# Where the RG-LRU pieces of the output projection stand among the attention heads, and when the second half of W_out is loaded

## The chip, the core and the metric

The kernel runs on one core of a Trainium2 chip. The metric is the device time of one execution in microseconds (us): the median of the runs. Five engines work side by side, each on its own instructions in a fixed order: PE (TensorE, the matmuls), DVE (VectorE), ACT (ScalarE), POOL (GpSimd) and SP (SyncE, which here only issues transfers). A wait of one engine for another is a semaphore.

## The reference

One block of a streaming encoder with a sequence of 1024 tokens and a model width of 1024, all in float32:

```python
x   = layer_norm(alpha*x + 0.5*swiglu(x, ffn1...))
z   = x @ w_in                                    # q, k, v, lru input, lru gate, forget gate
fox = forgetting_attention(q, k, v, fg)           # 8 heads of 64, causal
#     logit[t,s] = q_t.k_s/8 + cum_t - cum_s ;  softmax over s <= t ;  times v
lru = gelu(z_gate) * rg_lru(conv(z_x))            # 512 channels
x   = layer_norm(alpha*x + concat([fox, lru]) @ w_out)
x   = layer_norm(alpha*x + 0.5*swiglu(x, ffn2...))
```

The change sits in the line with `w_out`: the product has an lru half (rows 512 to 1023 of `w_out`) and a fox half (rows 0 to 511).

## The kernel before, in words

Every float32 product is made of three fp32r matmuls (`mm3`, L151 to L153) on operands that were split into a high and a low part: ACT copies the high part, DVE subtracts it from the source to get the low part. The two feed-forward blocks take most of the time and are not touched. Between them stand the input projection with the RG-LRU (`mixer_in`) and `attention`.

`attention` walks over 64 units. A unit is one head `h` and one block `i` of 128 query rows, which looks at `i + 1` blocks of keys; heads 0 to 5 take `i` from 7 down to 0, so unit number n is head n // 8 for the first 48, and units 48 to 63 mix heads 6 and 7. At step n of the loop stand, in this order:

- `probs` for unit n: score matmuls into a PSUM tile `s` of two (L967, L968); on POOL an affine select that masks a block of `cum` (L971); on DVE the sum with `cum` and its minimum (L973, tile `p`, scalars `m`); on ACT the exponential with the row sum (L974); on DVE a reciprocal (L975); on POOL the scaling of `p` (L976).
- `to_pT` for unit n - 3: PE transposes `p` (L987), ACT and DVE split the result into `pt` (L991, L992).
- `values` for unit n - 4 where its `i` is even: PE multiplies `pt` with `v` (L1003), ACT and DVE put the result into `o` (L1006, L1007); after an odd head both are split into `mix` (L1010, L1011), and the pair's `mix` is stored to memory by POOL (L1014, `mix_d`).
- at some steps a piece of the lru half of the output projection: `down_tile` for one block of 128 rows and half of the columns. A piece is 12 matmuls of 128x512 (L151 to L153, `a<-w,mix`) and one DVE addition of the sum to the residual row (L213). There are 16 pieces. They stand at steps 0 and 1 and wherever n % 8 is 2, 3 or 4, until they run out at step 35:

```python
fill = [(i, d) for i in range(NT) for d in range(2)]
...
if fill and (n < 2 or n % 8 in (2, 3, 4)):
    i, d = fill.pop(0)
    with self.tc.issue_after(scores.ins) if n < 3 else nullcontext():
        self.down_tile(i, lru_tiles, 1.0, (d,))
```

- at steps 45, 47, 49 and 51 one step of `out_w` for the fox half of `w_out`: it loads 1 MB into one of two `raw` buffers (every second step) and splits 128 rows of it (ACT L143, DVE L144, 128x1024). The eight `ws` buffers that the splits write, and the eight `h` buffers into which `mix` comes back from memory (SP, L1062), hold the lru half until the last piece has read it.
- loads of the next head: q, kh, kl twice each, `cum`, `v` (SP, L950 to L955), into two sets of buffers.

From unit 57 on stand the pieces of the fox half (also L151 to L153), each pair followed by the layer norm of a row block; then the second feed-forward block, whose first weights (L255, `raw`) SP already loads during attention, when the `raw` buffers are free.

A scheduler that runs when the program is built puts the instructions of each engine into their final order; the text above gives it the sequence to start from. It may move a transfer or a transpose ahead or back by some units.

Of the kernel before, what the change touches and what calls it, by code (L numbers as in the profile page):

```python
# [24 lines left out]
FOX = 512  # L25
# [23 lines left out]
def f32(ap):  # L49
    return ap.bitcast(F32)  # L50


class Block:
# [866 lines left out]

    def out_w(self, w_out, row0):

        wv = w_out.rearrange("(f p) d -> p f d", p=P)
        for c in range(2):
            r = self.raw([P, 2, D])
            f0 = row0 // P + 2 * c
            self.nc.sync.dma_start(r, wv[:, f0:f0 + 2, :])
            for j in range(2):  # L930
                yield tuple(t[:, 0, :] for t in self.split_ws(r[:, j:j + 1, :], 1))

    def attention(self, w_out, mixp, ln, normed):

        nc, v = self.nc, self.nc.vector
        mm = nc.tensor.matmul
        lru_w, (last_hi, last_lo) = self.out_w(w_out, FOX), self.marks
        lru_tiles = list(zip(self.mix_lru[0:2], lru_w))
        with self.tc.issue_after(last_hi.ins), self.tc.issue_after(last_lo.ins):
            lru_tiles += list(zip(self.mix_lru[2:4], lru_w))  # L940
        with self.pool("att_p", 3) as pp, self.pool("att_t", 1) as tp, self.pool("att_pt", 6) as ptp, self.pool("att_qk", 2, side="right") as qkp:

            def load(h):
                vt = qkp.tile([P, NT, P], F32R, tag="v", name=self.nm("v"))
                cum = qkp.tile([P, T], F32, tag="cum", name=self.nm("cum"))
                q, kh, kl = (qkp.tile([P, T], F32R, tag=t, name=self.nm(t)) for t in ("q", "kh", "kl"))
                mine = slice(64 * (h % 2), 64 * (h % 2) + 64)
                for j in range(2):
                    rows = slice(64 * j, 64 * j + 64)
                    nc.sync.dma_start(f32(q[rows]), self.q_d[h // 2, j, mine, :])  # L950
                    nc.sync.dma_start(f32(kh[rows]), self.k_d[h // 2, 0, mine, :])
                    nc.sync.dma_start(f32(kl[rows]), self.k_d[h // 2, 1, mine, :])
                row = self.cum_d[h:h + 1, :]
                nc.sync.dma_start(cum, bass.AP(tensor=row.tensor, offset=row.offset, ap=[[0, P], [1, T]]))
                nc.sync.dma_start(f32(vt), self.v_d[h].rearrange("(j p) d -> p j d", p=P))  # L955
                return q, kh, kl, vt, cum

            def probs(h, i):

                q, kh, kl, _, cum = heads[h]  # L960
                n = (i + 1) * P
                ts = slice(i * P, n)
                s = self.s_tile()
                for bank in range((n + H - 1) // H):
                    c1 = min(max(n - bank * H, 256), H)
                    cols = slice(bank * H, bank * H + c1)
                    mm(s[:, bank, 0:c1], q[:, ts], kh[:, cols], start=True, stop=False)  # L967
                    scores = mm(s[:, bank, 0:c1], q[:, ts], kl[:, cols], start=False, stop=True)  # L968
                sf = s.rearrange("p b c -> p (b c)")
                p = pp.tile([P, T], F32, tag="p", name=self.nm("p"))  # L970
                nc.gpsimd.affine_select(cum[:, ts], cum[:, ts], pattern=[[-1, P]], compare_op=ALU.is_ge, fill=1e30, base=0, channel_multiplier=1)  # L971
                m = self.small.tile([P, 4], F32, tag="m", name=self.nm("m"))
                v.tensor_tensor_reduce(p[:, 0:n], sf[:, 0:n], cum[:, 0:n], 1.0, 3e38, ALU.add, ALU.min, m[:, 1:2])  # L973
                nc.scalar.activation(p[:, 0:n], p[:, 0:n], AF.Exp, bias=m[:, 1:2], scale=-1.0, accum_out=m[:, 2:3])  # L974
                v.reciprocal(m[:, 3:4], m[:, 2:3])  # L975
                nc.gpsimd.tensor_scalar(p[:, 0:n], p[:, 0:n], m[:, 3:4], 1.0, op0=ALU.mult, op1=ALU.mult)  # L976
                return p, scores

            def to_pT(h, i, p):
                if i % 2:  # L980
                    pts[h, i // 2] = [tuple(ptp.tile([P, 4, 256], F32R, tag="pt", name=self.nm("pt")) for _ in range(2))
                                      for _ in range((i + 4) // 4)]
                for g in range((i + 4) // 4):
                    js = range(4 * g, min(4 * g + 4, i + 1))
                    pa = self.a_tile()
                    for j in js:
                        nc.tensor.transpose(pa[:, (j % 4) * P:(j % 4 + 1) * P], p[:, j * P:(j + 1) * P], self.ident)  # L987
                    w = len(js)
                    pav = pa.rearrange("p (j t) -> p j t", j=4)[:, 0:w, :]
                    hi, lo = (x[:, 0:w, (i % 2) * P:(i % 2 + 1) * P] for x in pts[h, i // 2][g])  # L990
                    nc.scalar.copy(hi, pav)  # L991
                    v.tensor_tensor(lo, pav, f32(hi), ALU.subtract)  # L992

            def values(h, qt):
                vt = heads[h][3]
                b = h % 2
                rows, rest = slice(64 * b, 64 * b + 64), slice(64 - 64 * b, P - 64 * b)
                pv = self.a_tile()
                last = 2 * qt + 1
                for j in range(last + 1):  # L1000
                    ps = slice(P, 256) if j == last else slice(0, 256)
                    for l in range(2):
                        mm(pv[:, ps], vt[:, j, :], pts[h, qt][j // 4][l][:, j % 4, ps], start=j == 0 and l == 0, stop=j == last and l == 1)  # L1003
                cols = slice(qt * 256, (qt + 1) * 256)
                t = outs[h // 2]
                nc.scalar.copy(t[rows, cols], pv[rest, 0:256])  # L1006
                v.tensor_tensor(t[rows, cols], t[rows, cols], pv[rows, 0:256], ALU.add)  # L1007
                if b:
                    hi, lo = (x[:, cols] for x in mixes[h // 2])
                    nc.scalar.copy(hi, t[:, cols])  # L1010
                    v.tensor_tensor(lo, t[:, cols], f32(hi), ALU.subtract)  # L1011
                    if qt == 0 and h < HEADS - 1:
                        for l in range(2):
                            nc.gpsimd.dma_start(mix_d[h // 2][l], f32(mixes[h // 2][l]))  # L1014
# [3 lines left out]
            units = [(h, i) for h in range(HEADS - 2) for i in reversed(range(NT))]  # L1018
            units += [(6 + h, i) for h, i in ((0, 7), (0, 6), (0, 5), (0, 4), (1, 7), (1, 6), (0, 3), (0, 2),
                                              (1, 5), (1, 4), (0, 1), (0, 0), (1, 3), (1, 2), (1, 1), (1, 0))]  # L1020
            tiles, mix, w_fox, w_steps = [], [], [], self.out_w(w_out, 0)
            MIXES = 46, 48, 52
            fill = [(i, d) for i in range(NT) for d in range(2)]
            AHEAD = 3
            heads[0] = load(0)
# [8 lines left out]
            for n in range(len(units) + AHEAD + 1):  # L1034
                if n < len(units):
                    h, i = units[n]
                    if i == 5 and h < 6 or (h, i) == (6, 6):
                        heads[h + 1] = load(h + 1)
                    if i == NT - 1:
                        if h % 2 == 0:  # L1040
                            outs[h // 2] = tp.tile([P, T], F32, tag="o", name=self.nm("o"))
                        else:
                            mixes[h // 2] = tuple(mixp.tile([P, T], F32R, tag="h", name=self.nm("mix")) for _ in range(2))
                    ps[n], scores = probs(h, i)
                if 0 <= n - AHEAD < len(units):
                    to_pT(*units[n - AHEAD], ps.pop(n - AHEAD))
                if 0 <= n - AHEAD - 1 < len(units):
                    h, i = units[n - AHEAD - 1]
                    if i % 2 == 0:
                        values(h, i // 2)  # L1050
                        if h == HEADS - 1:
                            tiles += [(i + 1, 0), (i + 1, 1), (i, 0), (i, 1)]
                if fill and (n < 2 or n % 8 in (2, 3, 4)):
                    i, d = fill.pop(0)
                    with self.tc.issue_after(scores.ins) if n < 3 else nullcontext():
                        self.down_tile(i, lru_tiles, 1.0, (d,))
                if 45 <= n < 53 and n % 2:
                    w_fox.append(next(w_steps))
                if n in MIXES:
                    mix.append(tuple(self.hp.tile([P, T], F32R, tag="h", name=self.nm("mix")) for _ in range(2)))  # L1060
                    for l in range(2):
                        nc.sync.dma_start(f32(mix[-1][l]), mix_d[len(mix) - 1][l])  # L1062
                    if len(mix) == 3:
                        self.load_gb(*ln, [self.hp.tile([P, T], F32, tag="h", name=self.nm("gb")) for _ in range(2)])
                if tiles:
                    out_tile()
# [134 lines left out]
```

## Time and profile before

| | us |
|---|---|
| median of 3 runs | 2349.59 |
| lowest to highest | 2349.21 to 2351.27 |
| profiled execution, its own time | 2347.14 |
| its span, first to last instruction | 2345.4 |
| PE busy in the span | 2304.1 |
| DVE busy | 1631.6 |
| ACT busy | 1011.6 |
| POOL busy | 223.5 |

The profiled execution is 2.45 us below the median of the timed runs. Between its span and its own time lie 1.74 us. The heads' score matmuls start at 1209.02 us of the span (head 1) and the first piece of the fox half starts at 1343.03 us. In this text a head's time runs from the first score matmul of its first unit to that of the next head's.

### The profile page before, as it was taken

How to read it: one execution, taken by the hardware profiler on the slowest of the kernel's cores; microseconds unless marked ns; L12 is line 12 of the kernel's file. 1: busy time of each engine (PE TensorE's matmuls, PEld its weight loads, DVE VectorE, ACT ScalarE, POOL GpSimd, SP SyncE). 2: the span in 40 equal slices, each digit the busy share in tenths (PEclk: the TensorE clock that was granted, in tenths of full speed). 3: DMA queues.
4: the chain of work that ended last, by engine and by line, in shares of the span. 5: the costliest groups of instructions: out<-in, count | busy, mean ns of one | idle time of the engine just before them, and what ended most of it. 6: DMA issues, size and time to landing. Idle time of an engine off the chain costs nothing.

```text
span 2345.4 us, 28311 instructions
## 1 busy us (share of the span) xinstructions
PE 2304.1 (98%) x10721; PEld 1915.8 (82%) x10721; DVE 1631.6 (70%) x2512; ACT 1011.6 (43%) x1587; POOL 223.5 (10%) x364
## 2 busy tenths in 40 slices
PE   9999999999999999999999899999999999999997
PEld 7788888888888888888888777888888888788886
DVE  7766565666567888866667899665656566468787
ACT  5443333433344345454556745433333343344341
POOL 0020000000000000011134410000000000000000
PEclk9999999999999999999999999999999999999999
DMA  3433232323376434132366812232323232564532
GB/s 116 144 88 122 96 120 86 117 86 117 132 254 209 168 108 127 55 109 91 113 185 156 231 63 82 98 117 86 122 95 121 86 117 86 201 247 155 196 108 90
DMA packets 175832, 298.93 MB, mean 127 GB/s; under 512 B 8192, under 2 KB 100672, under 8 KB 175696
## 3 DMA queue, kind: packets, MB, share of 16 engines
q1 hardware_dynamic: 152624, 218.15, 29.1%
q0 software_dynamic: 23072, 78.97, 9.1%
q8 instruction: 84, 1.38, 0.3%
q14 instruction: 52, 0.43, 0.1%
HBM read 214.22 MB, written 82.87 MB: 127 GB/s over the span
## 4 chain that ended last, share of the span: by engine, by line
PE 87%; DVE 5%; issue 4%; DMA 2%; ACT 1%; POOL 1%; SPq 0%; POOLq 0%; ACTq 0%; DVEq 0%
PE x L153 9%; PE x L151 9%; PE x L152 9%; PE b L152 7%; PE b L153 7%; PE b L151 7%; PE s L153 6%; PE s L152 6%; PE s L151 6%; PE a L152 5%; PE a L151 5%; PE a L153 5%; PE a L1003 1%; PE a L987 1%; PE s L967 1%
## 5 line engine op out<-in xcount | busy, mean ns | idle before, releaser
L273 ACT CAST ws<-t 128x512 fp32r<-128x512 f32 x240 | 148.9, 623 | 389.3 <-PE b L152 268.8
L273 ACT CAST ws<-raw 128x512 fp32r<-128x512 f32 x180 | 111.8, 623 | 259.0 <-PE x L152 257.8
L274 DVE TENSOR_TENSOR ws<-raw,ws 128x512 fp32r<-128x512 f32 x180 | 123.9, 688 | 142.8 <-ACT ws L273 139.4
L274 DVE TENSOR_TENSOR ws<-t,ws 128x512 fp32r<-128x512 f32 x240 | 164.4, 686 | 70.5 <-ACT ws L273 68.5
L151 PE MATMUL b<-As,ws 128*128 128x512 f32 x512 | 199.8, 390 | 2.8 <-ACT As L309 2.6
L151 PE MATMUL a<-ws,ws 128*128 128x512 f32 x512 | 199.2, 390 | 2.1 <-ACT ws L607 1.6
L151 PE MATMUL x<-As,ws 128*128 128x512 f32 x512 | 199.6, 390 | 1.1 <-ACT ws L273 1.0
L153 PE MATMUL x<-As,ws 128*128 128x512 f32 x512 | 199.4, 390 | 0.7 <-DVE ws L274 0.6
L152 PE MATMUL a<-ws,ws 128*128 128x512 f32 x512 | 199.5, 390 | 0.5 <-DVE ws L608 0.5
L152 PE MATMUL b<-As,ws 128*128 128x512 f32 x512 | 199.4, 389 | 0.2 <-DVE As L315 0.2
L153 PE MATMUL b<-As,ws 128*128 128x512 f32 x512 | 199.4, 389 | 0.0
L152 PE MATMUL x<-As,ws 128*128 128x512 f32 x512 | 199.2, 389 | 0.0
L153 PE MATMUL a<-ws,ws 128*128 128x512 f32 x512 | 199.2, 389 | 0.0
L153 PE MATMUL x<-A,ws 128*128 128x512 f32 x496 | 193.2, 390 | 0.9 <-DVE ws L315 0.7
L151 PE MATMUL x<-A,ws 128*128 128x512 f32 x496 | 193.2, 389 | 0.8 <-ACT ws L273 0.8
L152 PE MATMUL x<-A,ws 128*128 128x512 f32 x496 | 193.0, 389 | 0.0
L607 ACT CAST ws<-raw 128x1024 fp32r<-128x1024 f32 x112 | 117.4, 1050 | 161.3 <-PE a L152 87.6
L543 POOL DMA_DIRECT2D h_d<-row x96 | 69.0, 721 | 1157.1 <-DVE row L537 1118.0
L608 DVE TENSOR_TENSOR ws<-raw,ws 128x1024 fp32r<-128x1024 f32 x112 | 136.5, 1220 | 53.9 <-ACT ws L607 53.0
L151 PE MATMUL s<-ws,ws 128*128 128x512 f32 x384 | 149.5, 389 | 0.0
L153 PE MATMUL s<-ws,ws 128*128 128x512 f32 x384 | 149.4, 389 | 0.0
L152 PE MATMUL s<-ws,ws 128*128 128x512 f32 x384 | 149.4, 389 | 0.0
(248 smaller groups left out, 5229.9 us busy)
## 6 DMA issues: line engine op xcount, KB each, us to landing
raw<-h_d SPq DMA_DIRECT2D x56, 1024.0 KB, 5.5
h_d<-row POOLq DMA_DIRECT2D x96, 512.0 KB, 3.7
wd<-in_ffn_w_down_dram SPq DMA_DIRECT2D x32, 1024.0 KB, 7.8
raw<-in_ffn_w_gate_dram SPq DMA_DIRECT2D x30, 1024.0 KB, 5.4
raw<-in_ffn_w_up_dram SPq DMA_DIRECT2D x30, 1024.0 KB, 5.4
h_d<-row POOLq DMA_DIRECT2D x32, 256.0 KB, 2.7
raw<-in_w_in_dram SPq DMA_DIRECT2D x16, 512.0 KB, 5.2
row<-in_x_dram SPq DMA_DIRECT2D x12, 512.0 KB, 8.9
```

Of the source, the lines that this page charges most:

```text
L151: mm(out, ah, bh, start=first, stop=False, skip_group_check=goes_on)
L152: mm(out, ah, bl, start=False, stop=False, skip_group_check=goes_on)
L153: mm(out, al, bh, start=False, stop=last, skip_group_check=goes_on)
L273: nc.scalar.copy(hi, src)
L274: v.tensor_tensor(lo, src, f32(hi), ALU.subtract)
L543: nc.gpsimd.dma_start(d[:, 2 * n:2 * n + 2], t.rearrange("p (r t) -> p r t", r=2))
L607: nc.scalar.copy(hi, src)
L608: self.mark = v.tensor_tensor(lo, src, f32(hi), ALU.subtract)
L967: mm(s[:, bank, 0:c1], q[:, ts], kh[:, cols], start=True, stop=False)
L987: nc.tensor.transpose(pa[:, (j % 4) * P:(j % 4 + 1) * P], p[:, j * P:(j + 1) * P], self.ident)
L1003: mm(pv[:, ps], vt[:, j, :], pts[h, qt][j // 4][l][:, j % 4, ps], start=j == 0 and l == 0, stop=j == last and l == 1)
```

## The change

The 16 pieces get a list of steps of their own: `FILLS`. Steps 0 to 4 keep their pieces; the other eleven stand at 8, 12 and 15 (head 1), 19 and 22 (head 2), 26 and 29 (head 3), 33 and 36 (head 4), 40 and 43 (head 5), where before they stood at 10, 11 and 12, 18, 19 and 20, 26, 27 and 28, 34 and 35. The loading of `w_out` is taken out of `out_w`; the fox half's two loads are written at steps 10 and 17 instead of 45 and 49, and its splits stay at 45, 47, 49 and 51.

```diff
-    def out_w(self, w_out, row0):
+    def out_raws(self, w_out, row0):
...
             self.nc.sync.dma_start(r, wv[:, f0:f0 + 2, :])
+            yield r
+
+    def out_w(self, raws):
+
+        for r in raws:
             for j in range(2):
                 yield tuple(t[:, 0, :] for t in self.split_ws(r[:, j:j + 1, :], 1))
...
-        lru_w, (last_hi, last_lo) = self.out_w(w_out, FOX), self.marks
+        lru_w, (last_hi, last_lo) = self.out_w(self.out_raws(w_out, FOX)), self.marks
...
-            tiles, mix, w_fox, w_steps = [], [], [], self.out_w(w_out, 0)
+            tiles, mix, w_fox, fox_raws = [], [], [], []
+            fox_loads, w_steps = self.out_raws(w_out, 0), self.out_w(fox_raws)
             MIXES = 46, 48, 52
+            FILLS = 0, 1, 2, 3, 4, 8, 12, 15, 19, 22, 26, 29, 33, 36, 40, 43
...
-                if fill and (n < 2 or n % 8 in (2, 3, 4)):
+                if n in (10, 17):
+                    fox_raws.append(next(fox_loads))
+                if n in FILLS:
                     i, d = fill.pop(0)
```

The line numbers of the changed kernel are 5 higher in this part of the loop (L967 becomes L972, and so on), and 9 higher from the place of the pieces on (L1062 becomes L1071).

On SP the two loads of the fox half (`raw`, L929) keep the rows that they had: the first stands ahead of head 0's loads, the second ahead of head 2's, in both kernels. What moves on SP is what stands around the loads of heads 6 and 7 (the two sets that follow each other from here; in both kernels `v` ends a head's set). SP before, from the `v` of head 6 to the `cum` of head 7, with the second feed-forward block's weights between them:

```order
L955 DMA v_10840<-v_d 128x8x128
L255 DMA raw_12046<-in_ffn_w_gate_dram 128x4x256
L255 DMA raw_12047<-in_ffn_w_up_dram 128x4x256
L255 DMA raw_12046<-in_ffn_w_gate_dram 128x4x256
L950 DMA q_11086<-q_d 64x1024
L951 DMA kh_11087<-k_d 64x1024
L952 DMA kl_11088<-k_d 64x1024
L950 DMA q_11086<-q_d 64x1024
L951 DMA kh_11087<-k_d 64x1024
L952 DMA kl_11088<-k_d 64x1024
L954 DMA cum_11085<-cum_d 128x1024
```

SP of the change, the same place:

```order
L960 DMA v_10830<-v_d 128x8x128
L1071 DMA mix_11015<-mix_d 128x1024
L1071 DMA mix_11016<-mix_d 128x1024
L1071 DMA mix_11082<-mix_d 128x1024
L1071 DMA mix_11083<-mix_d 128x1024
L956 DMA kh_11089<-k_d 64x1024
L955 DMA q_11088<-q_d 64x1024
L957 DMA kl_11090<-k_d 64x1024
L955 DMA q_11088<-q_d 64x1024
L956 DMA kh_11089<-k_d 64x1024
L957 DMA kl_11090<-k_d 64x1024
L959 DMA cum_11087<-cum_d 128x1024
```

Between the sets of heads 6 and 7 stood three weight loads, and now four loads of `mix`, which before stood ahead of head 6's set. The weight loads stand behind head 7's `cum`.

On DVE the splits of the fox half (L144) stood behind the score rows of units 35, 37, 39 and 42, and stand behind those of units 43, 45, 47 and 50. DVE before, from just behind the score row of unit 51 to that of unit 52, the first of head 7 (its operand is `s_11204`):

```order
L975 RECIPROCAL m_11146<-m_11146 128x1
L992 TENSOR_TENSOR pt_11170<-a_11173,pt_11169 128x4x128
L975 RECIPROCAL m_11164<-m_11164 128x1
L992 TENSOR_TENSOR pt_11172<-a_11180,pt_11171 128x4x128
L1007 TENSOR_TENSOR o_10498<-o_10498,a_11187 64x256
L992 TENSOR_TENSOR pt_11170<-a_11218,pt_11169 128x4x128
L1011 TENSOR_TENSOR mix_10787<-o_10498,mix_10786 128x256
L992 TENSOR_TENSOR pt_11172<-a_11225,pt_11171 128x3x128
L992 TENSOR_TENSOR pt_11255<-a_11258,pt_11254 128x4x128
L992 TENSOR_TENSOR pt_11257<-a_11265,pt_11256 128x2x128
L1007 TENSOR_TENSOR o_11059<-o_11059,a_11270 64x256
L973 ISA p_11209,m_11213<-s_11204,cum_11085 128x1024
```

DVE of the change, the same place:

```order
L978 ISA p_11160,m_11164<-s_11155,cum_10831 128x640
L978 ISA m_11164 128x1
L997 TENSOR_TENSOR pt_11170<-a_11173,pt_11169 128x4x128
L1012 TENSOR_TENSOR o_10474<-o_10474,a_11187 64x256
L997 TENSOR_TENSOR pt_11170<-a_11218,pt_11169 128x4x128
L980 RECIPROCAL m_11164<-m_11164 128x1
L997 TENSOR_TENSOR pt_11172<-a_11180,pt_11171 128x4x128
L1016 TENSOR_TENSOR mix_10763<-o_10474,mix_10762 128x256
L978 ISA p_11209,m_11213<-s_11204,cum_11087 128x1024
```

Head 7's first score row has moved up past the second half of unit 49's `pt`, both of unit 50's and one addition to `o`.

On PE the pieces of heads 1 to 5 stand apart from each other. PE before in head 1, around the transposes of unit 9 (L987 reading `p_9621`), with the end of one piece ahead of unit 12's score rows and the start of the next piece:

```order
L152 MATMUL a_9732<-w_9274,mix_8643 128x512
L153 MATMUL a_9732<-w_9273,mix_8644 128x512
L967 MATMUL s_9746<-kh_9365,q_9364 128x512
L968 MATMUL s_9746<-kl_9366,q_9364 128x512
L987 MATMUL a_9758<-ident,p_9621 128x128 x4
L987 MATMUL a_9765<-ident,p_9621 128x128 x3
L151 MATMUL a_9771<-w_9259,mix_7245 128x512
L152 MATMUL a_9771<-w_9260,mix_7245 128x512
```

PE of the change, around the same transposes (L992 reading `p_9635`):

```order
L1008 MATMUL a_9727<-pt_9644,v_9292 128x256
L972 MATMUL s_9734<-kh_9365,q_9364 128x512
L1008 MATMUL a_9727<-pt_9645,v_9292 128x256
L1008 MATMUL a_9727<-pt_9644,v_9292 128x128
L1008 MATMUL a_9727<-pt_9645,v_9292 128x128
L973 MATMUL s_9734<-kl_9366,q_9364 128x512
L992 MATMUL a_9746<-ident,p_9635 128x128 x4
L972 MATMUL s_9773<-kh_9365,q_9364 128x384
L992 MATMUL a_9753<-ident,p_9635 128x128 x3
L973 MATMUL s_9773<-kl_9366,q_9364 128x384
L151 MATMUL a_9759<-w_9259,mix_7245 128x512
L152 MATMUL a_9759<-w_9260,mix_7245 128x512
```

A piece no longer ends just ahead of these transposes: the one ahead is that of unit 8, and the one behind starts after unit 13's score rows.

## Rows read from the trace of the kernel before

**Rows 1.** The page: the span, the busy time of PE and DVE (share of the span, instructions), and the chain of work that ended last by engine.

```profile
span 2345.4 us, 28311 instructions
PE 2304.1 (98%) x10721; PEld 1915.8 (82%) x10721; DVE 1631.6 (70%) x2512; ACT 1011.6 (43%) x1587; POOL 223.5 (10%) x364
PE 87%; DVE 5%; issue 4%; DMA 2%; ACT 1%; POOL 1%; SPq 0%; POOLq 0%; ACTq 0%; DVEq 0%
```

**Rows 2.** Busy time by stretch: heads 1, 2, 3, 4, 5, and from head 6's first score matmul to the first piece of the fox half. The length, then busy us and instructions of PE, PE's weight loads, DVE, ACT and POOL, the granted PE clock (1.00 is 2.4 GHz), the DMA engines' busy share, GB/s.

```profile
1209.02:1231.00 21.98, 21.81 (x137) 19.32 (x137) 16.27 (x44) 13.41 (x33) 8.28 (x17) 1.00 0.50 121
1231.00:1253.24 22.24, 21.94 (x137) 19.37 (x137) 17.77 (x48) 14.60 (x38) 9.71 (x19) 1.00 0.60 166
1253.24:1275.22 21.98, 21.80 (x137) 19.31 (x137) 16.27 (x44) 13.40 (x33) 8.29 (x17) 1.00 0.52 121
1275.22:1296.09 20.87, 19.58 (x124) 16.95 (x123) 18.48 (x48) 16.64 (x39) 10.29 (x18) 1.00 0.82 231
1296.09:1313.49 17.40, 14.94 (x101) 12.73 (x102) 16.31 (x44) 14.46 (x36) 10.42 (x18) 1.00 1.03 276
1313.49:1343.03 29.54, 24.80 (x157) 21.13 (x157) 23.14 (x61) 21.05 (x50) 13.76 (x26) 0.94 0.82 228
```

**Rows 3.** Instructions of PE in order of time: the first matmul of one piece and the score matmul behind its last. Start, duration (pipelined, so longer than the step to the next), in brackets the idle time before and what ended it.

```profile
1214.86 0.40 PE L151 MATMUL a<-w,mix 128*128 128x512 f32 x1
...
1217.60 0.39 PE L967 MATMUL s<-kh,q 128*128 128x512 f32 x1
```

**Rows 4.** Instructions of PE in order of time: waits of heads 4 to 7 (a head's first score matmul, transposes, `values`, and scores again).

```profile
1296.09 0.50 PE L967 MATMUL s<-kh,q 128*128 128x512 f32 x1 [0.47 <-DVE m L973]
...
1303.84 1.09 PE L987 MATMUL a<-ident,p 128*128 128x128 f32 x8 [0.51 <-POOL p L976]
...
1306.40 0.66 PE L987 MATMUL a<-ident,p 128*128 128x128 f32 x4 [0.54 <-POOL p L976]
...
1309.75 1.34 PE L1003 MATMUL a<-pt,v 128*128 128x256 f32 x9 [0.86 <-DVE pt L992]
...
1323.93 0.47 PE L967 MATMUL s<-kh,q 128*128 128x512 f32 x1 [0.95 <-issue]
...
1325.44 0.47 PE L968 MATMUL s<-kl,q 128*128 128x512 f32 x1 [0.37 <-DMA kl<-k_d]
...
1331.49 0.50 PE L967 MATMUL s<-kh,q 128*128 128x512 f32 x1 [1.48 <-DVE m L973]
...
1333.10 0.55 PE L967 MATMUL s<-kh,q 128*128 128x384 f32 x1 [0.88 <-DVE m L973]
```

**Rows 5.** The chain that ended last, in order of time, around head 7's load: start, us, what.

```profile
1316.03 9.28 DMA kl<-k_d
...
1330.22 1.21 DVE p L973
```

**Rows 6.** Busy time by stretch as in rows 2, around the last two waits of rows 4.

```profile
1326.60:1330.00 3.40, 3.40 (x29) 3.14 (x28) 1.96 (x5) 1.39 (x4) 1.42 (x3) 1.00 1.07 378
1330.00:1333.28 3.28, 0.93 (x4) 0.48 (x4) 3.28 (x8) 2.14 (x5) 0.46 (x2) 1.00 0.67 219
1333.28:1336.69 3.41, 3.41 (x13) 2.76 (x14) 0.97 (x5) 2.23 (x5) 3.15 (x5) 0.50 0.66 241
```

**Rows 7.** Instructions of DVE and POOL in order of time: two splits of the fox half and the scaling on POOL beside each, then a scaling of the same two sizes with no split beside it.

```profile
1294.49 1.21 DVE L144 TENSOR_TENSOR w<-raw,w 128x1024 fp32r<-128x1024 f32 x1
1294.74 1.41 POOL L976 TENSOR_SCALAR p<-p,m 128x384 f32<-128x384 f32 x1 [0.55 <-DVE m L975]
...
1304.03 2.32 POOL L976 TENSOR_SCALAR p<-p,m 128x896 f32<-128x896 f32 x1
1304.25 1.21 DVE L144 TENSOR_TENSOR w<-raw,w 128x1024 fp32r<-128x1024 f32 x1
...
1312.50 0.59 POOL L976 TENSOR_SCALAR p<-p,m 128x384 f32<-128x384 f32 x1 [0.18 <-DVE m L975]
...
1321.32 1.02 POOL L976 TENSOR_SCALAR p<-p,m 128x896 f32<-128x896 f32 x1
```

**Rows 8.** SP's queue in order of time, start and us: the first load of head 6's set; the weight load ahead of head 7's set; the first of that set, its second `kl` and its `cum`; the two loads of the third pair's `mix`.

```profile
1296.42 0.45 SPq L951 DMA_DIRECT2D kh<-k_d  x1
...
1306.98 2.07 SPq L255 DMA_DIRECT2D raw<-in_ffn_w_gate_dram  x1
1312.98 0.45 SPq L950 DMA_DIRECT2D q<-q_d  x1
...
1316.03 0.59 SPq L952 DMA_DIRECT2D kl<-k_d  x1
...
1316.72 1.48 SPq L954 DMA_DIRECT2D cum<-cum_d  x1
...
1330.78 1.55 SPq L1062 DMA_DIRECT2D mix<-mix_d  x2
```

**Rows 9.** Transfers: size of one, median us from issue to landing. The first two rows are those issued between 1208 and 1213 us (head 2's set), the last is the third pair's `mix`.

```profile
kl<-k_d SPq DMA_DIRECT2D x2, 256.0 KB, 5.8
cum<-cum_d SPq DMA_DIRECT2D x1, 512.0 KB, 7.6
...
mix<-mix_d SPq DMA_DIRECT2D x2, 512.0 KB, 4.1
```

**Rows 10.** POOL in order of time: the first mask of head 6's `cum`.

```profile
1309.19 0.29 POOL L971 TENSOR_SCALAR_AFFINE_SELECT cum<-cum 128x128 f32<-128x128 f32 x1 [1.70 <-DMA cum<-cum_d]
```

## The prediction

> **What bounds the kernel now.** I read the page first: PE is busy for 98% of the span and makes up 87% of the chain that ended last [rows 1]. So a change that takes no work from PE can only win time in which PE waits or runs slowly. Next, busy time by head [rows 2]: heads 1 to 3 hold three pieces each and PE idles 0.17, 0.30 and 0.18 us in them. From head 4 on it idles: 1.29 us in head 4, 2.46 in head 5, 4.74 from there to the first piece of the fox half. Last, PE's own waits there [rows 4]. In heads 4 and 5 they end on DVE's score minimum (L973), on POOL's scaling (L976) and on the split of `pt`: without a piece between them the units come faster than DVE, ACT and POOL finish one. At 1323.93 and 1325.44 PE waits for head 7's load; the chain holds 9.28 us of its second `kl` [rows 5]. Unit 52 reaches DVE only at 1330.22, and the two longest waits follow (1.48 and 0.88 us). Right behind, PE's clock falls to 1.2 GHz (0.50) for 3.41 us, after 3.28 us in which PE was busy for 0.93 [rows 6].
>
> **The price of a piece and of a bare head.** A piece takes 1217.60 - 1214.86 = 2.74 us of PE [rows 3]. Heads 1 to 3 take 22.07 us on average; less three pieces (8.22) and 0.22 of idle time, a bare head is 13.63 us of PE [rows 2]. What a head takes above 13.63 plus its pieces I call its stall: 0.22 in heads 1 to 3; 20.87 - 13.63 - 5.48 = 1.76 in head 4 (two pieces); 17.40 - 13.63 = 3.77 in head 5 (none).
>
> **The change part by part.**
> Loads of W_out written at steps 10 and 17: nothing. Their rows on SP don't move, as the order shows. The work that hides them is the same as before.
> The pieces: the same 16 x 12 matmuls and 16 additions, so PE's work stays. From the start of head 1 to the first piece of the fox half PE took 87.07 + 17.40 + 29.54 = 134.01 us [rows 2]. I rebuild that stretch in three parts.
>
> Part one, heads 1 to 4, now with 9 pieces: 4 x 13.63 + 9 x 2.74 = 79.18 us, and the stalls. A two-piece head of this kind isn't in the trace. From below, it stalls 0.22 like a three-piece head; from above, 1.76 like head 4, which also had two of the four W_out splits and its two pieces side by side, with an empty run behind them. The splits are gone from here, and the longest run without a piece is four units, as in three-piece heads it was five. But units such as 9 have lost the piece that stood between their scores and their transposes (the order on PE). I take 0.65 per head, nearer the lower row: 2.60, together 81.78 (80.1 to 86.2).
>
> Part two, head 5, now with two pieces and three of the splits: 13.63 + 5.48 and head 4's stall of 1.76, with 0.24 more for a third split: 21.11, where 17.40 stood. Both parts together are 102.89 us against 104.47: 1.58 us won.
>
> Part three, head 6 to the first fox piece, 29.54 us before. Out: the waits 0.95, 0.37, 1.48 and 0.88 and half of the 3.41 us at 1.2 GHz, 1.70: 5.38 us [rows 4, 6]. They go if head 7's data come in time. Before, its set was issued from 1312.98 on behind 1.5 MB of weights, whose last issue ends at 1309.05 [rows 8], with the DMA engines 1.03 busy in head 5 [rows 2]; `kl` landed 9.28 us after issue, where 5.8 is the undisturbed median [rows 9]. Now four `mix` loads (2 MB) stand there instead. They wait for the buffers that the last piece reads, at unit 44, three units or 3/8 of 13.63 = 5.1 us of PE work ahead of the end of unit 47, which lets head 7's set go. 2 MB moved at head 5's 276 GB/s take 7.6 us, at the 378 of rows 6 5.5: most of it is over when head 7's set is issued, and the weights stand behind its `cum`. DVE's score row of unit 52 no longer stands behind five rows of `pt` of units 49 and 50 or an `o` (the order on DVE). In: the run without pieces, which was units 36 to 57, is now units 45 to 57, and one split with the backlog of the other three enters it. By head 5, whose stall of 3.77 came from such a run, I put 3.00 here. Sum: 29.54 - 5.38 + 3.00 = 27.16. From below, DVE's own work is 23.14 [rows 2] and one split of 1.21 [rows 7], 24.35; from above nothing goes and 3.00 comes, 32.54.
>
> 102.89 + 27.16 = 130.05, against 134.01: **3.96 us less**. From the first fox piece on the order of all engines is the same, so the rest moves as a block. Cover that this needs: the fox pieces read the third pair's `mix`, and its two loads now come behind the three later weight loads. Before, they were issued by 1332.33 [rows 8], 10.70 us ahead of the fox piece, and landed in 4.1 [rows 9]; 1.5 MB more ahead of them is 5.7 us at 276 GB/s, if none of it has moved by then. That leaves 0.9 us at worst and 6.6 at best; if the cover is gone, each us late is a us lost.
>
> The sum is made against the profiled execution (span 2345.4 us, its own time 2347.14, which is 2.45 below the median of the runs). I take 3.96 from the median: 2349.59 - 3.96 = 2345.6 us. 0.2%, 4.7 us, is about what a measurement of this kernel can tell from no change; the forecast lies just inside.
>
> **A rule weighed.** Beside a split (L144), which reads two SBUF tiles, POOL's scaling takes 1.41 us where 0.59 is usual and 2.32 where 1.02 is, while the split keeps its 1.21, also where the scaling had started first [rows 7]. So POOL pays 0.82 to 1.30 per split, and the four splits of both kernels cancel in my sum. The Trainium skill, SBUF — State Buffer, section Who interferes with whom, says that a VectorE instruction with two SBUF inputs contends with a GpSimd instruction that reads SBUF, and that whichever issues second is blocked until the first has finished. The trace agrees that they collide and disagrees on who pays: at 1304.03 the first one did. By the rule as written the cost could fall on DVE, which the sum doesn't have; that is the third rival.
>
> **The rivals.**
> 1. All of it goes: heads 1 to 4 stall 0.22 each, head 5 1.0, and part three takes 26.0, DVE's 24.35 and 1.65 that I add for the chain of its first unit. 80.06 + 20.11 + 26.0 = 126.2, 7.8 less: 2341.8. For it: pieces two or three units apart hide more than three in a row do. Against it: DVE has 19 to 20 us of rows in a head with two pieces and three splits (16.27 in head 1 [rows 2] less a piece's addition plus 3 x 1.21). 18%.
> 2. The wait only moves. Head 7's set still comes late behind the `mix` loads, the clock falls again: part three is 32.54, the sum 135.43, 1.4 more: 2351.0. For it: 1.70 us of POOL's time went to the landing of head 6's `cum` alone [rows 10], and the new four transfers are larger than the three weight loads that they replace. Against it: 5 us of lead. 14%.
> 3. The splits pay on DVE: two of four come second to a scaling of 1024 or 896 elements and wait about 1.1 us each, in the stretch where DVE sets the pace: 2.3 less won, 2347.9. The rule above says it; rows 7 speak against. 5%.
> 4. Slower: the transposes in heads 1 to 4. In a run without pieces PE comes to a unit's transposes before POOL has scaled it, as at 1303.84 and 1306.40 [rows 4], and in PE's order the next piece stands behind them and can't help. It costs 4 us for each us of stall per head: at 1.64 the gain is gone, at 2.82 the kernel is over 0.2% slower, at 3.0 it takes 2355.0. For it: head 5's 3.77. Against it: head 4's 1.76 with two splits in it. 8%.
> That the change does nothing where it says so is true of the loads of W_out, in every case.
>
> **How the numbers follow.** Forecast 55%, with a range of its own from 2343.4 to 2347.8; rivals 18, 14, 5 and 8%. Above 0.2% faster (below 2344.9) lies four tenths of the forecast (22%) and rival 1: 40%. The rest of the forecast (33%) and rivals 2 and 3 (19%) are within 0.2%: 52%. Rival 4: 8%. The range runs from rival 1's time to rival 2's and leaves out half of rival 1, part of rival 2 and all of rival 4: 2342.0 to 2350.6.
>
> **What would show it.** Heads 1 to 4 (to head 5's first score matmul) take 81.8 us, and head 5 about 21.1. Head 7's first scores wait for no load, DVE reaches unit 52 within 3 us of them, and the waits of 1.48 and 0.88 are gone; the clock stays at 1.00 from head 6 to the first fox piece, which comes 130 us after head 1's start. The splits stretch POOL's scalings next to units 43 to 50. Wrong would be: waits on POOL or DVE at each head's second unit's transposes; a `kl` or `cum` of head 7 that lands over 9 us after issue; fox pieces that wait for `mix`; a clock of 0.50 again.

## The result and the profile after

The changed kernel took 2352.57 us (median of 20 runs, 2347.66 to 2354.17) where the kernel before, run beside it, took 2349.40 (20 runs, 2345.76 to 2351.76): 1.0013 times as long, 95% interval 1.0007 to 1.0019. The forecast was 3.96 us less, and by the medians it became 3.17 us more. The profiled execution of the changed kernel has a span of 2351.7 us, its own time is 2353.41. In the experiments below the ratios leave out three single runs of 6 to 12 ms (one of e3, one of e4, one of the kernel before that ran beside e1 to e4), which the medians still count, so a ratio there isn't exactly the quotient of the two medians beside it.

The page of after, to be held against [rows 1]: the work is the same, the share of PE in the chain nearly so. The page alone doesn't tell where the 3 us are.

```profile
span 2351.7 us, 28325 instructions
PE 2311.1 (98%) x10721; PEld 1918.9 (82%) x10721; DVE 1632.6 (69%) x2512; ACT 1011.1 (43%) x1587; POOL 222.5 (9%) x364
PE 88%; DVE 6%; issue 2%; ACT 2%; DMA 1%; POOL 1%; SPq 0%; POOLq 0%; DVEq 0%; ACTq 0%
```

Busy time by stretch in after, with the columns of [rows 2]: heads 1 to 5, then head 6 to the first fox piece.

```profile
1211.78:1231.42 19.64, 19.36 (x125) 17.08 (x125) 15.44 (x43) 13.17 (x33) 8.25 (x17) 1.00 0.56 135
1231.42:1255.65 24.23, 23.51 (x148) 20.59 (x148) 19.01 (x53) 15.96 (x42) 10.14 (x20) 1.00 0.58 158
1255.65:1275.24 19.59, 18.71 (x116) 15.74 (x115) 14.37 (x39) 12.12 (x29) 7.65 (x15) 1.00 0.52 128
1275.24:1295.06 19.82, 19.58 (x125) 17.03 (x125) 16.58 (x46) 14.18 (x36) 9.48 (x19) 1.00 0.68 186
1295.06:1315.74 20.68, 19.65 (x124) 16.87 (x124) 17.01 (x44) 15.54 (x34) 8.86 (x16) 1.00 0.79 230
1315.74:1343.93 28.19, 24.40 (x157) 19.96 (x158) 25.16 (x60) 21.76 (x51) 12.89 (x23) 1.00 0.92 274
```

Heads 1 to 4 hold 2, 3, 2 and 2 pieces in these windows (the piece of step 15 is run after head 2's first scores) and take 83.28 us, head 5 takes 20.68, the last stretch 28.19: 132.15, against 134.01 before. So up to the fox pieces the change did win, 1.86 us between these two traces. (Head 1 starts 2.76 us later than in [rows 2], and these count in the 6.3 us between the two spans. They are no part of the change: in the ten profiled executions of this study head 1 starts anywhere from 1209.02 to 1213.35 us, in e2, which keeps the order of before, at 1213.22. From 1188 to 1196 us the granted clock is 0.79 on average both in after and in e2, and 1.00 in before.)

The loss stands behind the point where the forecast stopped looking. PE's first fox pieces in after, in order of time, with its wait:

```profile
1343.93 0.45 PE L151 MATMUL a<-w,mix 128*128 128x512 f32 x1
...
1345.83 0.39 PE L153 MATMUL a<-w,mix 128*128 128x512 f32 x1
1349.26 0.50 PE L151 MATMUL a<-w,mix 128*128 128x512 f32 x1 [3.04 <-ACT mix L1015]
```

Nine matmuls run, on the `mix` of heads 0 to 5. The tenth needs the fourth pair's, heads 6 and 7, and PE stands for 3.04 us. Busy time around it, columns of [rows 2]:

```profile
1343.93:1349.26 5.33, 2.29 (x12) 1.56 (x11) 2.11 (x7) 1.69 (x4) 3.28 (x5) 1.00 0.09 35
1349.26:1352.67 3.41, 3.41 (x13) 2.63 (x14) 2.56 (x7) 1.08 (x3) 0.37 (x2) 0.72 0.00 0
1352.67:1360.00 7.33, 7.33 (x39) 6.28 (x38) 4.93 (x13) 4.25 (x8) 0.41 (x1) 0.90 0.00 0
```

Behind the wait the granted clock is 0.72 and then 0.90, that is, part of the time at 1.2 GHz instead of 2.4, while PE is busy without a gap: 0.28 x 3.41 + 0.10 x 7.33 = 1.69 us lost. Balance: -1.86 + 3.04 + 1.69 = **+2.87 us**, where the medians say +3.17.

What makes the fourth pair's `mix` late is found by going back. ACT's L1015 (1348.80) waits for DVE's sum in `o`, and this for ACT's copy of a product of `values` (L1011, 1347.95). PE had ended that product by 1344.10; the copy is late because on ACT it stands behind the exponential of a later unit, unit 57, and this waits for DVE's score row at 1346.13. The score row waits for a mask on POOL, and the mask stands behind another instruction of POOL. So `mix` needs nothing of unit 57; it stands behind it in the fixed order of the engines. In after, first POOL, then SP, then DVE, then ACT (start, us, idle time before and what ended it):

```profile
1330.67 1.16 POOL L1019 DMA_DIRECT2D mix_d<-mix  x2
...
1344.80 1.05 POOL L180 TENSOR_SCALAR gb<-gb 128x1024 f32<-128x1024 f32 x1 [4.47 <-DMA gb<-in_ln_g_dram]
1345.80 0.30 POOL L976 TENSOR_SCALAR_AFFINE_SELECT cum<-cum 128x128 f32<-128x128 f32 x1
```

```profile
1327.86 0.82 SPq L255 DMA_DIRECT2D raw<-in_ffn_w_up_dram  x1
1336.12 1.53 SPq L1071 DMA_DIRECT2D mix<-mix_d  x2
1337.72 0.42 SPq L90 DMA_DIRECT2D gb<-in_ln_g_dram  x1
```

```profile
1346.13 0.82 DVE L978 CUSTOM_DVE_ANT_0 p<-s,cum 128x640 f32<-128x640 f32 x1 [3.62 <-POOL cum L976]
```

```profile
1347.00 0.83 ACT L979 ACTIVATE p<-p,m 128x640 f32<-128x640 f32 x1 [4.19 <-DVE m L978]
...
1347.95 0.36 ACT L1011 COPY o<-a 64x256 f32<-64x256 f32 x1
```

`gb` is the gain of the layer norm behind the fox pieces. POOL changes its sign (L180) as soon as it is loaded, and everything later on POOL stands behind that. The same places in the kernel before, POOL, SP and DVE:

```profile
1326.61 1.12 POOL L1014 DMA_DIRECT2D mix_d<-mix  x2 [1.12 <-ACT mix L1010]
...
1339.90 1.05 POOL L180 TENSOR_SCALAR gb<-gb 128x1024 f32<-128x1024 f32 x1 [2.12 <-DMA gb<-in_ln_g_dram]
```

```profile
1332.38 0.42 SPq L90 DMA_DIRECT2D gb<-in_ln_g_dram  x1
```

```profile
1341.80 0.82 DVE L973 CUSTOM_DVE_ANT_0 p<-s,cum 128x640 f32<-128x640 f32 x1 [0.18 <-POOL cum L971]
```

POOL waited here before too, 2.12 us, and DVE already lost 0.18 us by it, PE nothing: the cover was used up. The lead of `gb`'s issue over the first fox piece was 1343.03 - 1332.38 = 10.65 us and is 1343.93 - 1337.72 = 6.21, so 4.44 less. Of these, 1.35 come from the fox piece being earlier (28.19 against 29.54 us after head 6's start), 1.81 from the store of the third pair's `mix` standing later (14.93 against 13.12 us after head 6's start), and 1.28 from a longer way from this store to the loads that wait for it (5.45 against 4.17 us), beside the weight loads that now stand there.

### The profile page after: what moved, and what is told of

Read it like the earlier page. It is cut to its first block, busy times and chain, and to the rows that moved or that the text cites. A ratio compares the mean times of both kernels' runs of the same rounds, so it can differ in the third digit from the quotient of the medians.

```text
span 2351.7 us, 28325 instructions
## 1 busy us (share of the span) xinstructions
PE 2311.1 (98%) x10721; PEld 1918.9 (82%) x10721; DVE 1632.6 (69%) x2512; ACT 1011.1 (43%) x1587; POOL 222.5 (9%) x364
## 4 chain that ended last, share of the span: by engine, by line
PE 88%; DVE 6%; issue 2%; ACT 2%; DMA 1%; POOL 1%; SPq 0%; POOLq 0%; DVEq 0%; ACTq 0%
PE x L153 10%; PE x L151 9%; PE x L152 9%; PE b L152 7%; PE b L153 7%; PE b L151 7%; PE s L152 6%; PE s L153 6%; PE s L151 6%; PE a L151 5%; PE a L152 5%; PE a L153 5%; PE a L1008 1%; PE a L992 1%; DVE row L198 1%
```

## The experiments

**e1: the sign on POOL taken away.** The same result without L180: the sign goes into two constants of the layer norm on DVE, no instruction is added. Lines behind it are 1 lower.

```diff
-        self.nc.gpsimd.tensor_scalar(gb[0], gb[0], -1.0, 1.0, op0=ALU.mult, op1=ALU.mult)
-        v.tensor_scalar(w, mv[:, 1:2], EPS, 0.5, op0=ALU.add, op1=ALU.mult)
+        v.tensor_scalar(w, mv[:, 1:2], EPS, -0.5, op0=ALU.add, op1=ALU.mult)
-        v.scalar_tensor_tensor(y, w, 1.5, y, op0=ALU.subtract, op1=ALU.mult)
+        v.scalar_tensor_tensor(y, w, 1.5, y, op0=ALU.add, op1=ALU.mult)
```

> The changed kernel without the POOL instruction that multiplies the gain row gb by -1 (L180); the sign is taken into two constants of the layer norm instead, so that no instruction is added. All other rows of all engines stay. Theory A (the change loses because gb lands late, POOL stands 4.47 us at L180, the mask of unit 57 behind it comes late, DVE waits 3.62 us for the mask and PE 3.04 us for mix, after which its clock falls): that wait and the fall to 1.2 GHz behind it go, 3.04 + 1.7 = 4.7 us less than the changed kernel, 1.5 less than before, ratio to before 0.9994. Theory B (the loss lies in attention's order itself or in the part behind it): ratio as of the changed kernel, 1.0013, and PE waits 3 us for mix at another releaser.

Measured: 2347.49 us against 2351.05 of the kernel before, ratio 0.9985 (0.9976 to 0.9994). `gb` is issued as late as in after, 6.20 us ahead of the fox piece, and nobody waits for it any more. The busy time of the first 8.58 us of fox pieces in e1:

```profile
1343.42:1352.00 8.58, 8.58 (x49) 7.39 (x49) 5.62 (x16) 3.87 (x10) 2.15 (x4) 1.00 0.05 21
```

PE is busy for all of it at clock 1.00. So the 3.04 us and the slow clock behind them both came from L180. The times behind the cut agree: from the first fox piece to the end of the span after takes 1007.77 us and e1 1003.18, 4.59 less, where the rows say 4.73. The changed order without that wait is faster than both kernels (after and e1 were each held against the kernel before, not against each other). Run again later (e5), the same kernel gave 2347.32 against 2350.56, ratio 0.9990 (0.9982 to 0.9999).

> The kernel of e1 once more, as the base for the three beside it, which each change one thing in it. If e1's ratio of 0.9985 was the kernel and not the day, it is 0.9978 to 0.9994 again; the first pieces of the fox half run without a gap.

**e2: the same edit in the kernel before.** It tells whether L180 cost anything before the change.

> The kernel before with the same edit as e1. Theory A: there POOL stood 2.12 us at L180, but DVE waited only 0.18 us for the mask behind it, so ratio 1.0000 (0.9998 to 1.0001). If it is 0.9993 or less, the gain of e1 isn't that of the wait which the change brought.

Measured: 2350.96 against 2351.05, ratio 0.9998 (0.9989 to 1.0007). Within the 0.1% or 2 us that the interval leaves, L180 was free before, and it cost about 5 us after (3.04 + 1.69 by the trace; the ratio of after lies 0.28% above that of e1, 6.6 us, and 0.23% above that of e5, 5.4 us): the edit is worth something only with the new order.

The trace of e2, whose order is that of before, shows the same mechanism by chance at another place, head 6's `cum`. POOL's mask waits 3.62 us for that load, where it was 1.70 in [rows 10], the next mask stands behind it, and DVE waits for the next mask:

```profile
1315.30 0.29 POOL L970 TENSOR_SCALAR_AFFINE_SELECT cum<-cum 128x128 f32<-128x128 f32 x1 [3.62 <-DMA cum<-cum_d]
```

```profile
1316.66 0.56 DVE L972 CUSTOM_DVE_ANT_0 p<-s,cum 128x384 f32<-128x384 f32 x1 [1.68 <-POOL cum L970]
```

Head 5 takes 19.04 us there instead of 17.40, and the stretch from head 1 to the first fox piece 134.93 instead of 134.01. So against the order of before the change wins 1.86 us by one trace and 2.78 by the other; in after POOL waits for no `cum` in these heads.

**e3: the three later weight loads behind `gb`.** L180 stays; on SP the second feed-forward block's first loads wait until `gb` is issued.

```diff
-        load(0)
-        load(1)
+        with blk.tc.issue_after(blk.fetched.ins):
+            load(0)
+            load(1)
```

> The changed kernel with the four loads of the second feed-forward block's first weights (2 MB) put behind the two gb loads on SP; no other row moves. Theory A1 (gb is late because 1.5 to 2 MB of weights stand ahead of it and beside the store of mix, which took 5.7 us to land and 4.2 in the kernel before): the store lands 1 to 1.5 us earlier and gb 2 to 3 us earlier, PE's wait falls from 3.04 to under 1 us, ratio 0.9995 to 1.0003. Theory A2 (gb is late because the mix store is issued late, by DVE's backlog): gb lands at most 0.5 us earlier, ratio 1.0010 to 1.0013.

Measured: 2348.06 against 2351.05, ratio 0.9989 (0.9980 to 0.9998). SP and POOL in e3:

```profile
1333.52 1.82 SPq L1071 DMA_DIRECT2D mix<-mix_d  x2
1335.39 0.42 SPq L90 DMA_DIRECT2D gb<-in_ln_g_dram  x1
```

```profile
1342.06 1.05 POOL L180 TENSOR_SCALAR gb<-gb 128x1024 f32<-128x1024 f32 x1 [1.86 <-DMA gb<-in_ln_g_dram]
```

```profile
1346.52 0.50 PE L151 MATMUL a<-w,mix 128*128 128x512 f32 x1 [0.44 <-ACT mix L1015]
```

With the weights out of the way the store's data is loadable 2.98 us after the store's issue (1330.54) instead of 5.45, `gb` is issued 2.20 us earlier after head 6's start, and PE's wait shrinks from 3.04 to 0.44. The wait follows `gb`'s arrival, with L180 left as it was: this reaches the same cause from another side. The ratio came out below the 0.9995 to 1.0003 of theory A1, with an interval that reaches into it. It also shows the change's part in it: those three loads stood ahead of head 7's set before, and the new order put them beside the store.

**e4: pieces spread, but none later than before.** Eleven pieces in heads 1 to 4 as before, two or three units apart, the last at 35.

```diff
-            FILLS = 0, 1, 2, 3, 4, 8, 12, 15, 19, 22, 26, 29, 33, 36, 40, 43
+            FILLS = 0, 1, 2, 3, 4, 8, 10, 13, 16, 18, 21, 24, 26, 29, 32, 35
```

> The changed kernel with the eleven pieces at steps 8, 10, 13, 16, 18, 21, 24, 26, 29, 32 and 35: spread, but done where they were done before, so the splits of W_out and the first four mix loads stand where they stood in the kernel before. Theory C (spreading wins in heads 1 to 4 and the late end gives it back): heads 1 to 4 stall as in the changed kernel, the run without pieces stays that of before, gb lands as before: 1 to 3 us less than before, ratio 0.9988 to 0.9996. Theory D (three pieces side by side hide as much as spread ones): ratio 1.0000 or over.

Measured: 2354.84 against 2351.05, ratio 1.0008 (0.9999 to 1.0018), so no gain and possibly a small loss. Its heads 1 to 4, columns of [rows 2]:

```profile
1210.12:1233.50 23.38, 22.64 (x138) 19.45 (x138) 16.70 (x45) 13.88 (x34) 8.46 (x17) 1.00 0.46 114
1233.50:1256.87 23.37, 22.30 (x137) 19.12 (x136) 17.25 (x47) 13.98 (x36) 9.57 (x18) 1.00 0.58 158
1256.87:1280.09 23.22, 22.48 (x138) 19.30 (x137) 16.45 (x45) 13.71 (x34) 8.30 (x17) 1.00 0.49 114
1280.09:1301.23 21.14, 19.43 (x125) 16.91 (x124) 18.26 (x47) 16.41 (x37) 10.22 (x18) 1.00 0.82 239
```

The same eleven pieces took 87.07 us in [rows 2], 87.07 again in e2, and take 91.11 here. Three pieces in a row cost a head 22.07 us on average, three pieces apart 23.32. So spreading by itself loses 4 us there. In after too heads 1 to 4 lose: 83.28 us, where 87.07 less the two pieces that went to head 5 (5.48) would be 81.59. What the change wins up to the fox pieces, it wins behind them: head 5 stalls 1.57 us instead of 3.77, and the last stretch takes 28.19 instead of 29.54; 2.20 + 1.35 - 1.69 = 1.86.

**e6 to e8, built on e5.** The wait on `gb` is out of all three. e6 puts only head 1's three pieces back in a row, e7 the pairs too; e8 leaves out the four subtractions of the fox half's splits, and with them the low part of `W_out`'s fox half.

```diff
-            FILLS = 0, 1, 2, 3, 4, 8, 12, 15, 19, 22, 26, 29, 33, 36, 40, 43
+            FILLS = 0, 1, 2, 3, 4, 10, 11, 12, 19, 22, 26, 29, 33, 36, 40, 43     # e6
+            FILLS = 0, 1, 2, 3, 4, 10, 11, 12, 18, 19, 26, 27, 34, 35, 42, 43     # e7
```

```diff
-            fox_loads, w_steps = self.out_raws(w_out, 0), self.out_w(fox_raws)
+            fox_loads, w_steps = self.out_raws(w_out, 0), self.out_w(fox_raws, False)   # e8
...
+                if not low:
+                    hi = self.wsp.tile([P, 4 * VW], F32R, tag="ws", name=self.nm("w"))[:, 0:D]
+                    self.nc.scalar.copy(hi, r[:, j, :])
+                    yield hi, hi
+                    continue
```

> Like e5, but the three pieces at steps 8, 12 and 15 stand in a row at 10, 11 and 12, as they did before the change; all others stay. In after, head 2 (whose window gets the piece of step 15 and the two of 19 and 22) took 24.23 us, 2.38 above 13.63 plus 3 x 2.74, where three in a row stalled 0.22. Theory that three pieces with gaps between them cost a head 1.2 to 2.2 us: head 1 takes 22.1 and head 2 19.6, together 41.7 against 43.87, so 2 us less than e5 (ratio about 0.9977 if e5's is 0.9985). Rival, head 2's stall belongs to head 2 (the load of W_out's second half lands there): head 2 still stalls over 1.5, the sum is 43 or more and e6 is within 1 us of e5.

Measured: 2348.50 against 2350.56, ratio 0.9994 (0.9985 to 1.0003). Heads 1 and 2 of e6:

```profile
1213.35:1235.33 21.98, 21.80 (x137) 19.30 (x137) 16.27 (x44) 13.41 (x33) 8.28 (x17) 1.00 0.51 121
1235.33:1257.29 21.96, 21.06 (x137) 18.48 (x136) 18.24 (x52) 15.91 (x42) 10.18 (x20) 1.00 0.64 172
```

Head 1 is back at its 21.98, but head 2 takes 21.96, not 19.6, and the sum of 43.94 is that of e5 (43.87). The theory falls: head 2's excess is not that of a third piece with gaps, and putting these three pieces in a row won nothing. Part of it isn't even a stall: its window holds 52 matmuls of `values` where head 1 of after, also with two pieces, has 41, and head 3's window has nine matmuls fewer in all (x116 against x125). Heads 2 and 3 have to be read together.

> Like e6, and the pairs too stand in a row, at 18 and 19, 26 and 27, 34 and 35, 42 and 43. Theory that what matters is a row of pieces at the head's longest units: the two-piece heads stall 0.2 to 0.4 instead of 0.5 to 0.7, 1 us less than e6. Rival, that a run of six units without a piece costs more than a gap: each of the four two-piece heads stalls 1 us or more (head 4 of before stalled 1.76 so), 2 to 4 us more than e6.

Measured: 2346.06 against 2350.56, ratio 0.9981 (0.9972 to 0.9990), the fastest kernel of this study that does all the work. Its heads 2 to 5:

```profile
1231.64:1251.63 19.99, 19.59 (x126) 17.17 (x125) 16.84 (x47) 14.52 (x38) 9.63 (x19) 1.00 0.66 184
1251.63:1271.37 19.74, 19.46 (x126) 17.08 (x125) 15.27 (x43) 13.37 (x33) 8.15 (x16) 1.00 0.56 134
1271.37:1291.39 20.02, 19.62 (x125) 17.19 (x125) 16.92 (x47) 14.55 (x38) 9.73 (x19) 1.00 0.68 184
1291.39:1312.14 20.75, 19.67 (x124) 16.89 (x123) 16.90 (x44) 15.69 (x34) 8.96 (x16) 1.00 0.78 229
```

Heads 1 to 4 take 81.73 us where e5's take 83.25, with the same nine pieces. Head 1 stalls 0.13, the two-piece heads 0.88, 0.63 and 0.91: less than the rival's 1 us, more than the theory's 0.4. The step from e6 to e7 is 1.99 us in heads 1 to 4. So a pair side by side, with six units in a row without a piece, is better in heads 2 and 3 (39.73 against 41.91 in e6) than a pair three steps apart; in head 4 it is 0.19 worse.

> Like e5, but the fox half's four splits have no subtraction on DVE: the high part stands for the low one in the product, so W_out's low part is left out there. Theory that DVE and POOL set the pace from head 5 to the fox pieces: four subtractions of 1.21 us and the stretching of POOL's scalings beside them are gone, 3 to 5 us less than e5 from head 5's start to the first fox piece (48.9 us in after). Rival, that the chain of units (scores, minimum, exponential, scaling, transposes) sets it there and the subtractions lie in its gaps: less than 1 us.

Measured: 2345.79 against 2350.56, ratio 0.9980 (0.9971 to 0.9988). Head 5, and head 6 to the first fox piece:

```profile
1295.78:1315.74 19.96, 19.67 (x125) 16.88 (x124) 15.01 (x41) 15.86 (x34) 8.15 (x16) 1.00 0.86 246
1315.74:1343.27 27.53, 24.11 (x157) 19.89 (x158) 24.03 (x62) 22.05 (x52) 13.14 (x25) 1.00 0.93 265
```

These take 0.70 and 0.65 us less than e5's 20.66 and 28.18. Four subtractions of 1.21 us, 4.84 of DVE's time, were worth 1.35 to PE: between the two expectations, nearer the one by which they lie in DVE's gaps. (The edit also leaves out the four low buffers, so the 1.35 isn't the subtractions' alone.)

## Why the prediction was wrong

**The step that failed** is "From the first fox piece on the order of all engines is the same, so the rest moves as a block", with its cover. The cover was worked out for `mix` alone (0.9 us at worst), and for `mix` it held: nine fox matmuls ran on it without a wait. But behind the `mix` loads on SP stands `gb`, which POOL waits for, and behind that wait stood a mask. The same order doesn't mean the same time where one instruction waits for a transfer that has moved by 4.44 us. The trace of before showed it: POOL's 2.12 us for `gb`, and DVE's 0.18 right behind, cover zero. Following the queue by one row more would have given a price: with the prediction's own worst case, the loads 5.7 us later, and DVE's 0.18 us of wait already there, up to 5.9 us of wait. The lead of `gb` fell by 4.44; DVE waited 3.62, PE 3.04, and the slow clock took 1.69. e1 and e3 show it. The wait alone is more than the 1.86 that the rest did win; wait and clock together, 4.73, are more than the 3.96 that it was to win. The 2.10 between these two lie in the three parts: 1.50 too little in the first, 0.43 too much in the second, 1.03 too little in the third.

**Part one** (81.78): 83.28, inside the bounds of 80.1 to 86.2, 1.50 too little. Head 1 stalled 0.53 and head 4 0.71, as the 0.65 says, but heads 2 and 3 together 2.86. The term was argued from the longest run of units without a piece, put at four; in the PE order shown ahead of the prediction it is five already in head 1 (units 9 to 13). e4 and e7 show that it is no measure: pieces side by side, with longer runs, came out better. Rival 4's mechanism is there (PE waits 0.53 us for POOL's scaling at a transpose, 1241.32) but small. PE's idle time in heads 1 to 4 is 2.12 us (1.94 before, 1.25 in e7); the rest of the stall of 4.10 shows in the windows as busy time. That doesn't make it work: at 1345.60 a 128x512 matmul is shown with 0.39 us and the next one starts 0.23 later, so up to 0.16 us of each wait counts as busy. Which short waits make up the stall stays open.

**Part two** (21.11): 20.68. Head 5 ran two splits (1308.82 and 1314.13), not three; the other two ran in head 6.

**Part three** (27.16): 28.19. Right: head 7's load is waited for no longer (`kl` landed 6.7 and `cum` 8.1 us after issue), the waits of 1.48 and 0.88 [rows 4] and the slow clock of [rows 6] are gone. PE's remaining waits there in after:

```profile
1324.50 1.09 PE L992 MATMUL a<-ident,p 128*128 128x128 f32 x8 [0.77 <-POOL p L981]
...
1327.95 0.50 PE L972 MATMUL s<-kh,q 128*128 128x512 f32 x1 [0.56 <-DVE m L978]
...
1332.19 0.50 PE L972 MATMUL s<-kh,q 128*128 128x512 f32 x1 [0.46 <-DVE m L978]
...
1334.95 0.33 PE L992 MATMUL a<-ident,p 128*128 128x128 f32 x1 [0.69 <-POOL p L981]
```

The term that was mis-sized is the 3.00 put in for the run without pieces. Without it the working gives 29.54 - 5.38 = 24.16, the stretch took 28.19, so 4.03 came in, 1.03 more. PE's idle time hides this: it went from 4.74 us to 3.79, where the working has 4.74 - 3.68 + 3.00 = 4.06, and the excess stands in the busy time, 24.40 instead of 24.80 - 1.70 = 23.10. It looks as if the clock had given back only 0.40 of its 1.70. But busy time counts short waits, and the starts tell another story. Eight transposes and the row behind them, in before at clock 0.50:

```profile
1334.79 1.91 PE L987 MATMUL a<-ident,p 128*128 128x128 f32 x8
1336.35 1.77 PE L1003 MATMUL a<-pt,v 128*128 128x256 f32 x12
```

The row behind the eight of 1324.50 in after, at clock 1.00:

```profile
1325.35 0.36 PE L1008 MATMUL a<-pt,v 128*128 128x256 f32 x1
```

From start to start 1.56 us and 0.85. Over the whole slow stretch of before, the steps from start to start exceed the usual ones of the same matmuls by about 1.7 us, an estimate from the starts in the two traces. So the 1.70 was about right, and what takes it up again lies in longer steps of PE outside that stretch. Short waits are the likely reading; for which engine is open. Wrong too: DVE reached unit 52 only 5.37 us after its first score matmul (1325.55 to 1330.92; 6.29 before), not within 3. The prediction had the score row freed of five rows of `pt` and an `o`; by the order on DVE it has moved up past three and one, and three rows of `pt`, an `o` and a `mix` still stand between it and unit 51's. In time it had eight other rows and two reciprocals to let pass first, a split of 1.67 among them.

**Of the rivals** none is what happened. The second has the right shape, a wait that moves and the clock behind it, but sought it at head 7's set. **The rule weighed**, from the Trainium skill, SBUF — State Buffer, section Who interferes with whom, says that whichever issues second is blocked, and did better in after than the row that spoke against it: there the instruction that started second paid in each of three meetings, POOL's scaling twice (1.41 and 1.20 us at 1314.39 and 1318.56), DVE's split once (1.67 instead of 1.21 at 1325.09, while POOL's scaling of 1324.67 kept its 1.02). Its price on DVE was 0.46 us, not the 2.3 of rival 3. Yet the row of [rows 7] was no accident: in e2 and e4, where the same scaling of 896 elements starts 0.22 us ahead of a split, it takes 2.32 us both times and the split keeps its 1.21. In after the scaling had a lead of 0.41. What decides between the two stays open.

**The loads of W_out** at steps 10 and 17 were costed at nothing. That was right: in the order of every engine, the change of the loads alone leaves every row where it was before, and that of the pieces alone gives every row of after. So all of the difference is that of the pieces, and no run of the loads alone was needed.

## What to carry to other kernels

When a transfer is moved on a queue, follow the queue on to the next transfers and ask of each who waits for it, on which in-order engine, and what stands behind that wait; an instruction that waits and is needed much later, as the sign of `gb`, belongs behind the urgent ones or away altogether. "The rest moves as a block" is a claim to be tested at the first wait behind the cut, and a wait that the trace already shows with an engine a fraction of a us behind it has no cover left. What it holds up need not depend on it: `mix` was late because it stood behind another unit on ACT and DVE. And PE's busy time doesn't tell work from short waits; where waits come close together, count from start to start.

## What the runs showed of the hardware

The way from the store of `mix` (POOL) to its loads (SP) was 2.98 us with no weight loads beside it (e3), 4.17 in before and 5.45 with three weight loads issued just ahead of it (after). The same code takes different times ahead of attention, with head 1 starting anywhere in 4.3 us; so two profiles are compared from a common instruction on, not from the span's start. And a filler of 2.74 us of PE work came out better in a row than apart in two comparisons: three in a row cost a head 22.07 us, three apart 23.32 (e4), and heads 1 to 4 with all pieces in rows took 81.73 (e7) against 83.25 (e5). In e6 head 1's three alone, put in a row, gave nothing (43.94 against 43.87 for heads 1 and 2), and head 4's pair was 0.19 worse in a row. I had expected the opposite, and which wait makes the difference isn't settled.
